# Gate stage of a streaming encoder step: h added by accumulating transfers, upper frames transposed by VectorE

## The chip, the core and the metric

The kernel runs on one core of one Trainium2 chip. A core has five engines with a queue of instructions each, which they work off strictly in order: TensorE (PE; matmuls, 128 x 128), VectorE (DVE), ScalarE (ACT), GpSimd (POOL) and SyncE (SP), and 16 DMA engines that move data between the on-chip memory (SBUF) and the device's memory. Matmuls write to PSUM, from which VectorE and ScalarE read. Transfers are issued by an engine's queue: here by SP, POOL and, for a few, ScalarE. The metric is the device time of one execution in microseconds, the median of the runs; the profile is of one more execution.

## What is computed

One layer of an encoder on 2048 prompt frames and 32 sample frames of width 1024. The part that matters here is the last step, the gate, and the norm behind it:

```
hn = rmsnorm(h, g_mix);  proj = hn @ w_in;  ... two mixers ...
h = h + concat[yA, yB] @ w_out
gate = sigmoid(rmsnorm(h, g_ple) @ w_ple_gate)
h = h + (p @ w_ple) * gate
y = rmsnorm(h, g_final)
```

Everything is in 32-bit floats. Each 32-bit operand of a product is split into a high and a low part, and three matmuls (high x high, high x low, low x high) make one exact enough.

## The kernel before

**Stages.** The projections and mixers run first, then the output product with `w_out`, which writes the new h to memory (`h_d`), then, from about 704 us, nine embedding products `p @ w_ple`, which write e to memory (`e_d`), and from about 729 us the gate. In the stretch of the embedding products the gate's weights are prepared by VectorE and ScalarE.

**Tiles and pairs.** h is cut into 16 tiles of 128 rows and one of 32. The gate takes the tiles in pairs (0 and 1, 2 and 3, ... 14 and 15). For a pair the product 256 x 1024 by 1024 x 1024 is cut into 2 x 2 blocks and done with seven block products in place of eight (`seven`, L273). Each of the seven is 12 matmuls of 128 x 512. The products accumulate in three PSUM banks X, Y and Z; between them ScalarE copies a bank aside (`carry`, L1571), and `out` (L1576) adds the copy back, takes the sigmoid on ScalarE with the row's norm factor `rs_h` as its scale, and multiplies it with e on VectorE. The order of products in a pair: X with block 11 (carry), Y with 12 (out of the upper left quarter), X with S2 (carry), Z with S1 (carry), X with S3 (out of the lower right), Z with S4 (out of the upper right), X with 22 (out of the lower left). The tile of the upper rows is complete after the sixth product, that of the lower rows after the seventh. A product that accumulates on a bank must wait until the carry or the sum before it has read that bank.

**Frames.** The products want h turned, with its columns on the partitions. `prep_g(i)` (L1732) makes the frames of a pair: the turned blocks a11, a12 (upper tile) and a21, a22 (lower tile), their combinations S1 to S4 (`comb`), and the high and low parts of seven of them (`put`, through `split`, L80: a cast on ScalarE and a subtraction on VectorE). The lower tile is read in quarters (`by_quarters`, L1507: four transfers of 32 rows, so that the four 32-row groups lie where a transpose of 32 x 32 blocks gives the turned tile) and turned in place by one VectorE instruction (`turned_here`, L1558). The upper tile is read by rows (`load_rows`, L393) and turned by `turned` (L1544): two copies on ScalarE, which put the columns in the same order, and eight transposes on TensorE into PSUM. The frames of pair i+2 are made while pair i is multiplied, at steps between the products (`following`).

**Closing a tile.** `out` adds e * gate onto the tile of h, which has been read from `h_d`. `done_g` (L1589) then sums the squares on ScalarE (`sumsq`, L92), has POOL compute the factor (two small instructions, `rstd_of`, L70), multiplies on VectorE and stores. The last pair (`last_pair`, L1613) has a handwritten end of its own and its own loads of h.

**Order.** The kernel's code gives a program order; a scheduler with its own estimates of durations orders the instructions within each engine's queue, apart from those pinned by `keep_in_program_order`. Tiles come from rings: `ya` has five buffers of 128 x 1024, `xh` four, `st` four of 128 x 512, `ss` three. A tile's load waits until the tile that had its buffer before is no longer read. Before the change `ya` holds the frames' rows and e, `xh` holds h.

## Time and profile before

| what | value |
|---|---|
| median of 3 runs | 909.32 us (908.84 to 909.93) |
| the profiled execution | 909.97 us, of which the span of the profile is 908.2 us |
| granted TensorE clock | 0.998 of full speed |
| TensorE busy 729.4 to 895.9 us (the gate) | all of it |
| transposes on TensorE | 72: 64 of 128 rows and 8 of 32 rows (the short tile) |

The profile tells for each engine when it was busy, in what line of the kernel, and for the idle time before an instruction which other engine or transfer ended it last. A busy TensorE alone does not say that it is the bound; the chain of waits does. It goes back from the last instruction to what released each step, and here it stays on TensorE from the output product to 899.75 us, with a tail of some 8 us on the other engines and the last stores. In names such as `x_g<-wg,g` the first is the PSUM bank, then the weights and the frames; `pth` is the bank of the transposes, `c_g` a carried copy.

### The profile page before, as it was taken

What the parts mean: (1) busy time and instruction counts of PE and PEld (TensorE: products, weight loads), DVE (VectorE), ACT (ScalarE), POOL (GpSimd) and SP (SyncE); (2) the same over time, 40 slices, a digit from 0 to 9 for tenths busy, and PEclk for the clock granted to TensorE, in tenths of its full rate; (3) what the DMA queues carried; (4) which work ended last, traced back from release to release, by engine and by line L of the source; (5) the groups of instructions that cost most, each with busy time, mean ns of one, the idle gap of its engine ahead of it and who ended that gap; (6) DMA issues with size and microseconds to landing.
All of it is one profiled execution on the core that took longest, in us unless ns stands there. A gap on an engine that the chain in (4) does not pass through costs nothing.

```text
span 908.2 us, 12176 instructions
## 1 busy us (share of the span) xinstructions
PE 893.2 (98%) x4174; PEld 722.8 (80%) x4174; DVE 702.4 (77%) x1158; ACT 460.1 (51%) x834; POOL 152.0 (17%) x290
## 2 busy tenths in 40 slices
PE   8999999999999999999999999999999999999996
PEld 6788888888888887877778886888887888778885
DVE  6899799897993688846667579965565988897885
ACT  7744554554453345533444376544434865565554
POOL 2210122222121123100000020221111211120012
PEclk9999999999999999999999999999999999999999
DMA  8255286857699666667745496787677965565554
GB/s 268 63 188 172 84 262 204 246 157 226 179 340 424 176 222 200 215 222 225 264 136 175 163 331 198 255 259 250 199 274 254 342 244 176 184 228 196 185 193 168
DMA packets 113387, 198.52 MB, mean 219 GB/s; under 512 B 13174, under 2 KB 70062, under 8 KB 112429
## 3 DMA queue, kind: packets, MB, share of 16 engines
q1 hardware_dynamic: 91309, 124.72, 42.5%
q0 software_dynamic: 19568, 68.62, 22.2%
q10 hardware_dynamic: 2448, 4.39, 1.3%
q8 instruction: 33, 0.54, 0.3%
q14 instruction: 29, 0.24, 0.1%
HBM read 132.53 MB, written 65.15 MB: 218 GB/s over the span
## 4 chain that ended last, share of the span: by engine, by line
PE 73%; issue 11%; DMA 8%; DVE 3%; ACT 2%; POOL 2%; POOLq 0%; DVEq 0%; ACTq 0%
PE x_g L185 9%; PE x_o L185 8%; PE x_zab L646 6%; PE x_zbv L646 6%; PE x_ch L646 6%; PE z_g L185 5%; PE z_o L185 4%; DMA raw_zab_0b<-in_w_in_dram 4%; PE z_zab L646 3%; PE z_ch L646 3%; PE z_zbv L646 3%; PE e L109 2%; PE y_g L185 2%; PE y_o L185 2%; DMA B<-p_d 2%
## 5 line engine op out<-in xcount | busy, mean ns | idle before, releaser
L185 PE MATMUL z_o<-wo,y_S 128*128 128x512 f32 x192 | 47.4, 389 | 0.0
L185 PE MATMUL x_o<-wo_T,y_S 128*128 128x512 f32 x192 | 46.4, 391 | 0.6 <-DVE c_o L1319 0.6
L646 PE MATMUL x_zab<-B,w_zab_S 128*128 128x512 f32 x192 | 46.8, 392 | 0.2 <-DVE w_zab_S L84 0.2
L185 PE MATMUL z_g<-wg,g_S 128*128 128x512 f32 x192 | 46.8, 391 | 0.0
L646 PE MATMUL z_zab<-B,w_zab_S 128*128 128x512 f32 x192 | 46.8, 391 | 0.0
L185 PE MATMUL x_o<-wo,y 128*128 128x512 f32 x192 | 45.2, 390 | 0.0
L646 PEld LDWEIGHTS x_zab<-B,w_zab_S 128*128 128x128 f32 x192 | 35.8, 188 | 8.8 <-DVE w_zab_S L84 0.6
L185 PEld LDWEIGHTS x_o<-wo_T,y_S 128*128 128x128 f32 x192 | 35.9, 188 | 8.7 <-DVE c_o L1319 1.3
L185 PEld LDWEIGHTS x_o<-wo,y 128*128 128x128 f32 x192 | 36.1, 188 | 7.7
L646 PEld LDWEIGHTS z_zab<-B,w_zab_S 128*128 128x128 f32 x192 | 35.8, 188 | 7.8 <-DVE w_zab_S L84 0.3
L185 PEld LDWEIGHTS z_o<-wo,y_S 128*128 128x128 f32 x192 | 36.0, 188 | 7.5
L646 PE MATMUL x_ch<-B,w_ch_S 128*128 128x512 f32 x168 | 41.9, 393 | 0.0
L185 PEld LDWEIGHTS z_g<-wg,g_S 128*128 128x128 f32 x192 | 35.8, 188 | 7.5 <-ACT c_g L1573 0.2
L646 PE MATMUL x_zbv<-B,w_zbv_S 128*128 128x512 f32 x168 | 40.9, 393 | 0.3 <-ACT zs L986 0.3
L646 PE MATMUL z_zbv<-B,w_zbv_S 128*128 128x512 f32 x168 | 40.5, 390 | 0.0
L646 PE MATMUL z_ch<-B,w_ch_S 128*128 128x512 f32 x168 | 40.4, 390 | 0.0
L646 PEld LDWEIGHTS x_zbv<-B,w_zbv_S 128*128 128x128 f32 x168 | 31.3, 188 | 8.0 <-ACT zs L986 0.7
L646 PEld LDWEIGHTS x_ch<-B,w_ch_S 128*128 128x128 f32 x168 | 31.3, 188 | 7.3 <-ACT U L986 0.4
L646 PEld LDWEIGHTS z_ch<-B,w_ch_S 128*128 128x128 f32 x168 | 31.6, 188 | 6.6
L646 PEld LDWEIGHTS z_zbv<-B,w_zbv_S 128*128 128x128 f32 x168 | 31.5, 188 | 6.5
L81 ACT CAST y_S<-y_fS 128x512 fp32r<-128x512 f32 x28 | 17.0, 620 | 28.1 <-PE x_o L185 12.2
L1319 DVE TENSOR_TENSOR c_o<-x_o,x 128x512 f32<-128x512 f32 x14 | 9.6, 689 | 21.8 <-PE x_o L185 21.8
(552 smaller groups left out, 2288.9 us busy)
## 6 DMA issues: line engine op xcount, KB each, us to landing
wn<-in_w_in_dram SPq DMA_DIRECT2D x24, 512.0 KB, 4.8
y<-y_d SPq DMA_DIRECT2D x16, 512.0 KB, 6.8
p_dT<-T POOLq DMA_DIRECT2D x15, 512.0 KB, 5.1
e<-e_d SPq DMA_DIRECT2D x15, 512.0 KB, 4.1
x<-in_x_prompt_dram SPq DMA_DIRECT2D x14, 512.0 KB, 5.6
B<-p_d POOLq DMA_DIRECT2D x3, 2048.0 KB, 15.6
B<-p_dT POOLq DMA_DIRECT2D x3, 2048.0 KB, 21.5
h_d<-x SPq DMA_DIRECT2D x12, 512.0 KB, 7.1
```

The source lines that it names most:

```text
L81: ins = nc.scalar.copy(hi, src)
L109: nc.tensor.matmul(ps, pps[:, a, k], wp[k][b][:, cs], start=k + q == 0, stop=k == 1 and q == 2)
L185: nc.tensor.matmul(ps[:n], lhs[:, k, a, :n], w[b][:, k], start=start and k + q == 0, stop=k == KH - 1 and q == 2, skip_group_check=True)
L646: nc.tensor.matmul(ps, lhs[:, k, x], b[:, k, y], start=start and k + q == 0, stop=stop and k == KH - 1 and q == 2, skip_group_check=True)
L1319: add = lambda o, a, b: nc.vector.tensor_tensor(o, a, b, op=ALU.add)
```

## The change

- h is no longer loaded for the pairs ahead of the last. `out` multiplies e by the gate in place, and when a tile's second half is done, an accumulating transfer on POOL's queue adds the tile's rows of `h_d` onto e. The 28 additions of these tiles on VectorE go.
- `done_g` of a pair's two tiles works on e, and moves into the next pair: at its step 4 (after product four) for the upper tile, at step 6 for the lower one; in the last pair at steps 3 and 4. The sum of squares and the multiplication are pinned there.
- e is read into `ya` (the first pair's into `xh`), the frames from tile 4 on into `xh`, and the frames' reads come at step 1.
- The upper tile is read in quarters too and turned by VectorE, pinned in program order. The 64 transposes on TensorE and the 16 copies on ScalarE go.
- The stores of tiles 6 to 11 move from SP's queue to POOL's.

```diff
-        def by_quarters(i):
+        def by_quarters(i, pool=ya):
             r, n = tiles[i]
-            t = ring4(ya, f"hn_{i}")
+            t = ring4(xh if i > 3 else pool, f"hn_{i}")
...
-            first_h = load_rows(xh, "hn", 0, h_d)
+            first_h = by_quarters(0, xh)
...
-                ee, hh = half_of(e, at, n), half_of(h, at, n)
+                ee = half_of(e, at, n)
                 nc.vector.tensor_tensor(ee, ee, c[:n], op=ALU.mult)
-                nc.vector.tensor_tensor(hh, hh, ee, op=ALU.add)
+                if h is not None:
+                    hh = half_of(h, at, n)
+                    nc.vector.tensor_tensor(hh, hh, ee, op=ALU.add)
+                elif at[0] + at[1] == 1:
+                    r = tiles[i + at[0]][0]
+                    nc.gpsimd.dma_start(e[at[0]], h_d[r:r + P], accum_op=ALU.add)
...
-            nc.vector.scalar_tensor_tensor(h[:n], h[:n], rf[:n], g_bc[:n], op0=ALU.mult, op1=ALU.mult)
-            (nc.sync if 6 <= i < NT - 1 else nc.gpsimd).dma_start(rows_of(y_p, y_s, r, n), h[:n])
+            ins = nc.vector.scalar_tensor_tensor(h[:n], h[:n], rf[:n], g_bc[:n], op0=ALU.mult, op1=ALU.mult)
+            if later:
+                tc.keep_in_program_order(ins)
+            (nc.sync if NT - 5 <= i < NT - 1 else nc.gpsimd).dma_start(rows_of(y_p, y_s, r, n), h[:n])
...
-            seven(f"g{i}", A, W, held, out, {1: chunk, 3: before, 4: rest, 5: upper_half}, first_tile=True, end=end)
+            seven(f"g{i}", A, W, held, out, {1: chunk, 3: sooner, 4: lambda: (before(), rest()), 5: upper_half}, first_tile=True, end=end)
...
-                got["upper"] = load_rows(ya, "hn", i, h_d) if i else first_h
+                got["upper"] = by_quarters(i) if i else first_h
...
+            def sooner():
+                if not ahead:
+                    load()
+
             def first():
-                if not ahead:
+                if not got:
                     load()
-                lower.extend(turned_here(got["lower"], not i))
+                lower.extend(turned_here(got["lower"], True))
...
-                a11, a12 = turned(i, got["upper"])
+                a11, a12 = turned_here(got["upper"], True)
...
-            return {2: first, 4 if i in (2, 8) else 3: second}
+            return {1: sooner, 2: first, 4 if i in (2, 8) else 3: second}
...
+        def joined(a, b):
+            def both(p, q):
+                def run():
+                    p()
+                    q()
+                return run
+            return {**a, **{st: both(a[st], f) if st in a else f for st, f in b.items()}}
...
-            h = [load_rows(xh, "h", i + b, h_d, queue=nc.gpsimd if i < 6 else nc.sync) for b in range(2)]
-            e = [load_rows(ya, "e", i + b, e_d) for b in range(2)]
-            seven(f"g{i}", A, W, *gate_ops(h, e, P, f"g{i}", i), following)
-            done_g(i, h[0])
+            e = [load_rows(ya if i else xh, "e", i + b, e_d) for b in range(2)]
+            if i:
+                following = joined(following, finish)
+            seven(f"g{i}", A, W, *gate_ops(None, e, P, f"g{i}", i), following)
+            finish = {st: lambda b=b, i=i, e=e: done_g(i + b, e[b], True) for b, st in enumerate((4, 6))}
             if i in (0, 2, 4):
                 next(short_steps)
-            if i + 2 < NT - 3:
-                done_g(i + 1, h[1])
-        last_pair(NT - 3, S[NT - 3], lambda: done_g(NT - 4, h[1], True))
+        last_pair(NT - 3, S[NT - 3], finish[4], finish[6])
```

How this moves instructions is seen at three places. In names like `g12_S2` the first number is the pair's upper tile. First TensorE, in the pair of tiles 10 and 11, from the fifth product on; before:

```order
L185 MATMUL x_g10_7546<-wg_T3_6494,g10_S3_7451 128x512 x12
L185 MATMUL z_g10_7548<-wg_21_6507,g10_S4_7454 128x512 x10
L1554 MATMUL pth_12_0_7603<-ident_75,ho_12_0_7604 128x128 x4
L1554 MATMUL pth_12_1_7610<-ident_75,ho_12_1_7611 128x128 x4
L185 MATMUL z_g10_7548<-wg_21_6507,g10_S4_7454 128x512 x2
L185 MATMUL x_g10_7546<-wq_6245,g10_22_7457 128x512 x12
```

and now:

```order
L185 MATMUL x_g10_7436<-wg_T3_6484,g10_S3_7346 128x512 x12
L185 MATMUL x_g12_7604<-wg_11_6219,g12_11_7496 128x512 x2
L185 MATMUL z_g10_7438<-wg_21_6497,g10_S4_7349 128x512 x12
L185 MATMUL x_g10_7436<-wq_6245,g10_22_7352 128x512 x12
L185 MATMUL x_g12_7604<-wg_11_6219,g12_11_7496 128x512 x10
```

The eight transposes are gone, and two matmuls of the next pair's first product stand ahead of the sixth product.

Second VectorE, in the pair of tiles 12 and 13, from the sum of its fifth product on; before:

```order
L1581 TENSOR_TENSOR c_g12_11_7840<-x_g12_7730,c_g12_11_7840 128x512
L1584 TENSOR_TENSOR e_13_7728<-e_13_7728,c_g12_11_7840 128x512
L1585 TENSOR_TENSOR h_13_7724<-h_13_7724,e_13_7728 128x512
L1560 STREAM_TRANSPOSE hn_15_7763<-hn_15_7763 128x1024
L1581 TENSOR_TENSOR c_g12_01_7783<-z_g12_7732,c_g12_01_7783 128x512
L1743 TENSOR_TENSOR g14_fS1_7785<-hn_15_7763 128x512
L1584 TENSOR_TENSOR e_12_7726<-e_12_7726,c_g12_01_7783 128x512
L84 TENSOR_TENSOR g14_11_7801<-pth_14_0_7787,g14_11_7801 128x4x128
```

and now:

```order
L1581 TENSOR_TENSOR c_g12_11_7703<-x_g12_7604,c_g12_11_7703 128x512
L84 TENSOR_TENSOR g14_S4_7685<-g14_fS4_7677,g14_S4_7685 128x4x128
L1581 TENSOR_TENSOR c_g12_01_7659<-z_g12_7606,c_g12_01_7659 128x512
L84 TENSOR_TENSOR g14_22_7688<-hn_15_7621,g14_22_7688 128x4x128
L1597 SCALAR_TENSOR_TENSOR e_10_7432<-e_10_7432,rstd_f10_7709,g_bc_89 128x1024
L1584 TENSOR_TENSOR e_13_7602<-e_13_7602,c_g12_11_7703 128x512
L1584 TENSOR_TENSOR e_12_7600<-e_12_7600,c_g12_01_7659 128x512
L1584 TENSOR_TENSOR e_13_7602<-e_13_7602,g_g12_10_7764 128x512
L1597 SCALAR_TENSOR_TENSOR e_11_7434<-e_11_7434,rstd_f11_7748,g_bc_89 128x1024
```

The frames of the next pair (the two transposes, the combinations and all but two of the splits) now stand ahead of the sum of the fifth product, and the multiplications that complete the tiles 12 and 13 come behind all of them and behind the closing of tile 10. The accumulating transfers follow the last two of these multiplications.

Third ScalarE, at the start of the last pair; before:

```order
L94 ACTIVATE junk_90,ssq_f12_7890<-h_12_7722 128x1024
L1573 COPY c_g14_01_7961<-x_g14_7908 128x512
L94 ACTIVATE junk_90,ssq_f13_7963<-h_13_7724 128x1024
L1666 ACTIVATE c_g14_00_7923<-c_g14_00_7923,rs_h_88 128x512
L1573 COPY c_g14_11_7983<-z_g14_7910 128x512
L1638 ACTIVATE junk_90,ssq_l0_0_7985<-h_14_7902 128x512
```

and now:

```order
L1673 ACTIVATE c_g14_00_7793<-c_g14_00_7793,rs_h_88 128x512
L1573 COPY c_g14_01_7831<-x_g14_7778 128x512
L94 ACTIVATE junk_90,ssq_f12_7833<-e_12_7600 128x1024
L1573 COPY c_g14_11_7853<-z_g14_7780 128x512
L94 ACTIVATE junk_90,ssq_f13_7855<-e_13_7602 128x1024
L1645 ACTIVATE junk_90,ssq_l0_0_7863<-h_14_7772 128x512
```

The squares of tile 12 stand between the copies of the third and of the fourth product, those of tile 13 behind the latter, and both read a tile that a transfer has completed.

More of the change, by code (lines that the diff above doesn't have):

```diff
@@ L1611, in short_ops, with last_pair @@
             return carry, out
-        def last_pair(i, A, before):
+        def last_pair(i, A, sooner, before):
             pps = load_pps(ss.tile([P, 2, 2, P], F32R, tag="s", name="pps_l"), i + 1, nc.sync)
@@ L1739, in put, with comb @@
                 split(view(A[q][:, :, 0]), view(A[q][:, :, 1]), src)
-            def comb(q, x, y, op, view=lambda t: t):
-                t = ss.tile([P, KH, P], F32, tag="s", name=f"g{i}_f{q}")
-                nc.vector.tensor_tensor(view(t), x, y, op=op)
+            def comb(q, x, y, op):
+                t = whole(ss.tile([P, KH, P], F32, tag="s", name=f"g{i}_f{q}"))
+                nc.vector.tensor_tensor(t, x, y, op=op)
                 return t
@@ L1749, in load, with first @@
                 got["lower"] = by_quarters(i + 1) if i else first_lower
-                got["upper"] = load_rows(ya, "hn", i, h_d) if i else first_h
+                got["upper"] = by_quarters(i) if i else first_h
             if ahead:
                 load()
-            def first():
+            def sooner():
                 if not ahead:
                     load()
-                lower.extend(turned_here(got["lower"], not i))
+            def first():
+                if not got:
+                    load()
+                lower.extend(turned_here(got["lower"], True))
             def second():
                 a21, a22 = lower
-                s1 = comb("S1", a21, a22, ALU.add, whole)
-                a11, a12 = turned(i, got["upper"])
-                put("11", a11)
+                s1 = comb("S1", a21, a22, ALU.add)
+                a11, a12 = turned_here(got["upper"], True)
+                put("11", a11, whole)
                 s2 = comb("S2", s1, a11, ALU.subtract)
-                s3 = comb("S3", whole(a11), a21, ALU.subtract, whole)
-                put("12", a12)
-                put("S2", s2)
+                s3 = comb("S3", a11, a21, ALU.subtract)
+                put("12", a12, whole)
+                put("S2", s2, whole)
                 s4 = comb("S4", a12, s2, ALU.subtract)
-                put("S1", s1)
-                put("S3", s3)
-                put("S4", s4)
+                put("S1", s1, whole)
+                put("S3", s3, whole)
+                put("S4", s4, whole)
                 put("22", a22, whole)
             S[i] = A
-            return {2: first, 4 if i in (2, 8) else 3: second}
+            return {1: sooner, 2: first, 4 if i in (2, 8) else 3: second}
         S = {}
```

## The prediction

> **What bounds the kernel now.** I read the page's busy table, then the chain of waits over the last 200 us in order of time. The chain (start, length, what) runs on TensorE without a break through the whole gate stage; this is the pair of tiles 6 and 7, then the first, the slowest and the last of the eight groups of transposes, and the last product:
>
> ```profile
> PE 893.2 (98%) x4174; PEld 722.8 (80%) x4174; DVE 702.4 (77%) x1158; ACT 460.1 (51%) x834; POOL 152.0 (17%) x290
> ...
> 718.71 0.87 PE pth L1554 x8
> ...
> 781.61 2.72 PE x_g L185 x12
> 784.33 0.46 PE z_g L185 x2
> 784.78 0.88 PE pth L1554 x8
> 785.66 2.31 PE z_g L185 x10
> 787.97 2.72 PE x_g L185 x12
> ...
> 854.06 1.03 PE pth L1554 x8
> ...
> 876.65 0.87 PE pth L1554 x8
> ...
> 899.75 0.73 PE e_l L109 x6
> ```
>
> A product of twelve matmuls takes 2.72 us, seven of them 19.04 us a pair, and a transpose group is simply wedged between them. So what TensorE no longer does comes off the end, as long as the other engines keep feeding it. The next view, busy time by stretches (length, then PE, PEld, DVE, ACT, POOL busy with counts, clock, DMA share, GB/s), says how much room they have: the stretch in which the embedding product hides the gate's weights, and one pair of the gate:
>
> ```profile
> 704.00:729.40 25.40, 25.40 (x117) 20.55 (x117) 24.83 (x40) 22.37 (x45) 7.23 (x15) 1.00 0.95 334
> ...
> 836.00:858.00 22.00, 22.00 (x102) 18.11 (x101) 18.95 (x28) 11.89 (x21) 2.07 (x4) 1.00 0.53 191
> ```
>
> VectorE is at 18.95 of 22 us in a pair, ScalarE at 11.89, and the transfers use about half of their engines. VectorE is the second bound, three microseconds a pair behind.
>
> **Removed from TensorE.** Eight groups of eight 128-row transposes leave it (the eight 32-row ones of the short tile stay). Six of the groups took 0.87, one 0.88, one 1.03: together 7.1 us, all on the chain. Nothing is added there. This is the whole gain on offer.
>
> **VectorE and ScalarE.** The groups by line over the gate stage:
>
> ```profile
> L1585 DVE TENSOR_TENSOR h<-h,e 128x512 f32<-128x512 f32 (+1 forms) x30 | 20.0, 684 | 0.8 <-DMA h<-h_d 0.6
> L1560 DVE STREAM_TRANSPOSE hn<-hn 128x1024 f32<-128x1024 f32 x8 | 9.9, 1238 | 0.0
> L1552 ACT COPY ho<-hn 128x512 f32<-128x512 f32 (+1 forms) x18 | 10.4, 619 | 3.4 <-DMA hn<-h_d 3.4
> ```
>
> 28 of the 30 additions go. Back to back they come every 0.60 us (two of them in a row of 1.28 below), so 2.4 us a pair. One more transpose a pair costs 1.24. VectorE is relieved by about 1.2 us a pair, TensorE's pair shrinks by 0.9: the room stays what it was. ScalarE loses two copies a pair, 16 of the 18. Both are off the chain and I count them at zero.
>
> In the embedding stretch VectorE is full (24.83 of 25.40), and there the added transpose has no removed addition beside it: all that follows is 1.2 us later. What would be late next is the lower weights' splits, which the second product wants. In the new order they stand behind the frames of the first pair; counted at 0.6 us each they end some 4 us before that product starts. Zero, and at worst 1.2 us if that cover is gone.
>
> **Order inside a pair.** This is the place where the new order is tighter. Old pair of tiles 8 and 9:
>
> ```profile
> 827.00 0.69 DVE L1584 TENSOR_TENSOR e<-e,c_g 128x512 f32<-128x512 f32 x1 [0.79 <-ACT c_g L1582]
> 827.61 1.24 DVE L1560 STREAM_TRANSPOSE hn<-hn 128x1024 f32<-128x1024 f32 x1
> ...
> 829.34 0.68 DVE L1743 TENSOR_TENSOR g_fS<-hn 128x512 f32<-128x512 f32 x1
> 832.74 0.69 DVE L84 TENSOR_TENSOR g<-pth,g 128x512 fp32r<-128x512 f32 x1 [2.71 <-ACT g L81]
> ...
> 834.05 1.66 ACT L81 CAST g_S<-g_fS 128x512 fp32r<-128x512 f32 x3 [0.86 <-DVE g_fS L1743]
> ...
> 841.14 1.28 DVE L1585 TENSOR_TENSOR h<-h,e 128x512 f32<-128x512 f32 x2
> ...
> 844.61 1.28 DVE L1592 SCALAR_TENSOR_TENSOR h<-h,rstd_f,g_bc 128x1024 f32<-128x1024 f32 x1 [0.17 <-POOL rstd_f L77]
> ```
>
> VectorE used to wait 2.71 us for TensorE's and ScalarE's turn of the upper frames; now it runs two transposes and nine operations in one go. From a pair's start: product two ends at 5.4, its sum, sigmoid and multiplication end at about 7.7, two transposes and nine operations take 2 x 1.24 + 9 x 0.60 = 7.9, and the sum of product five ends at 16.3. Product seven accumulates on that bank and starts at 16.3 plus whatever of the next pair's first product is put before it (2 to 11 matmuls). Just in time. On ScalarE, in the pairs of tiles 10 and 12, five casts now stand ahead of the copy of product four that product six waits for: cast one starts when the upper transpose ends, about 10.8, five at 0.52 apiece (three in a row of 1.66 with its tail) end at 13.4, the copy at 14.0, product six is due at 13.6 plus two matmuls, 14.1. I take 0.3 us for each of these two pairs: 0.6. Lower bound zero, upper bound 1 us in each of seven pairs.
>
> **The transfers.** The 14 loads of h become 14 accumulating transfers, all on POOL's queue, and each is now behind a multiplication and ahead of a tile's statistics. The nearest rows (last number: median us from issue to landing) are plain loads of the same size, and the quarters that the upper frames now use too:
>
> ```profile
> h<-h_d POOLq DMA_DIRECT2D x6, 512.0 KB, 5.2
> ...
> hn<-h_d SPq DMA_DIRECT2D x25, 128.0 KB, 2.9
> ...
> L396 POOL DMA_DIRECT2D h<-h_d x6: 527/532/577, 729.3 to 781.0; - x6
> ```
>
> No accumulating transfer is in this trace. Below, it lands like a plain load: 5.2. Above, it reads both operands and takes twice that: 10.4. The fixed part of the 5.2 is not doubled, so I take the middle, 7.8. The quarters cost nothing: they are read a pair ahead, 2.9 us each, into a ring that e no longer shares. On SP's queue a load of e now waits for the store of the tile five before it, and quarters stand behind it; by the order that store ends early in the pair before the one that wants the tile, over 10 us ahead. Behind a waiting accumulation on POOL stand the statistics and the store of the pair before, which are wanted only by the ring.
>
> When is it wanted? VectorE's order puts the multiplication that completes a pair's first tile about 20.5 us after that pair's start, 1.5 into the next; with 0.53 of issue it starts at 2.0. In the middle pairs its squares stand behind the copy of product four, at about 14.5: 12.5 us of room. In the last pair they stand behind the copy of product three:
>
> ```profile
> 886.52 0.59 ACT L1573 COPY c_g<-x_g 128x512 f32<-128x512 f32 x1 [1.33 <-PE x_g L185]
> 887.01 1.06 ACT L94 ACTIVATE junk<-h 128x1024 bf16<-128x1024 f32 x1
> ...
> 889.24 0.57 ACT L1573 COPY c_g<-z_g 128x512 f32<-128x512 f32 x1
> 889.89 2.97 PE L185 MATMUL z_g<-wg,g_S 128*128 128x512 f32 x12
> ```
>
> There that is 9.0 us after the pair's start, 7.0 of room. The second pair is as tight: the first pair's multiplication stands behind frames that started late behind the weights, some 6 us into the second pair by the same counting; its squares are due at 11.5, and the casts behind them have about 1.2 more before a product waits: 6.7, call it 7. What queues behind a late square on ScalarE is the copy of product four (last pair) or the frames' casts (second pair), and TensorE waits for both. I price each at landing time less 7: 0.8 twice, 1.6 us.
>
> The Trainium skill ("Collectives: The Full Stack", the bandwidth ceiling) says that an add in the transfer is slow not for the add but because it reads two sources, and gives about half the rate. By "DMA: Bandwidth & Descriptors" (anatomy of one DMA) a plain one of 512 KB would be 2.0 plus 1.2 us; doubling the second term gives an estimate of 4.4 in all, and the 1.6 us would be zero. The loads here show 5.2, so its fixed part is too small in this traffic, and no run here shows the add.
>
> **The sum.** Profiled execution 909.97 (span 908.20, 1.77 around it): 909.97 - 7.1 + 0.6 + 1.6 = 905.1. That execution lies 0.65 above the median of the runs, 909.32, so the forecast for the median is 904.4.
>
> **Rivals.** (a) The transfer lands within 7 us: only the 0.6 is lost, 902.8. For it: DMA engines half idle in the stage, and the plain loads' 5.2. Against it: two operands. By the skill's two pages this is the outcome. (b) Slower: the accumulating transfers land late. Each microsecond above 7 costs two in all, and above 12.5 also one in each of five middle pairs; 6.5 us of gain are gone at 10.3, and 0.2% is lost at about 11.2. At 14 us it is 909.3 - 6.5 + 14 + 7.5 = 924. For it: POOL's loads of h under the heavy traffic before the stage took a median of 9.3, and issue is serial with statistics and stores on POOL's queue. Against it: DMA share 0.53 in a pair.
>
> ```profile
> h<-h_d POOLq DMA_DIRECT2D x2, 512.0 KB, 9.3
> ```
>
> (c) No change: VectorE's unbroken run makes the sum of product five late by a microsecond in each of the seven pairs, and TensorE waits for it where it used to transpose: 909.3 - 7.1 + 7 = 909. For it: the margin above is nearly nothing. Against it: the next pair's matmuls that the order puts ahead of product seven, up to 2.5 us of cover. That the transposes stay is no rival: in the order of the changed kernel the 128-row ones are gone.
>
> **How the numbers follow.** Forecast 0.50 (903.2 to 907.5), (a) 0.25, (b) 0.13, (c) 0.12. A measurement of this kernel can tell about 0.2%, 1.8 us. Forecast and (a) are both faster: 0.75; (c) is the same: 0.12; (b) slower: 0.13. The range starts at full gain, 902.0, and reaches through (c) to 909.5; left out is (b).
>
> **What would show it.** Right: no 128-row transposes on TensorE and products of 2.72 us back to back; accumulating transfers landing within 6 to 9 us; TensorE's gaps, if any, at product six of the last pair and in the second pair, with squares of e as ScalarE's wait on a transfer. Wrong: landing times above 10 us and ScalarE waiting on them in every pair (b), or TensorE's product seven waiting for VectorE's sums (c), or a gap before the gate's first products, behind the weights' splits.

## The result, and the profile after

| | before | changed |
|---|---|---|
| median | 909.32 us (908.37 to 911.04, 7 runs) | 915.30 us (911.28 to 916.38, 7 runs) |
| ratio, 95% interval | | 1.0056 (1.0036 to 1.0075) |
| the profiled execution, and its span | 909.97, 908.2 | 916.35, 914.6 |
| TensorE's last product ends at (row start plus length) | 900.47 | 907.68 |

The change makes the kernel slower by about 0.6%, where 904.4 us was forecast. TensorE has lost its transposes and still ends 7.2 us later. The first view says where: what TensorE waited for in the whole execution (total, times, longest).

```profile
...
PE x_gl L337 <- DVE c_gl L1608: 2.3, 1, 2.3
PE x_g L1722 <- DVE c_g L1677: 2.0, 1, 2.0
PE e L109 <- ACT eout L167: 2.0, 1, 2.0
PE x_g L185 <- DVE c_g L1581: 1.4, 2, 0.9
...
PE z_g L185 <- ACT c_g L1573: 1.0, 1, 1.0
```

Before, TensorE was busy through all of the gate. Now it waits at six places from the embedding products on; the rows left out lie ahead of them. The timeline of TensorE (start, length, line, operation, count, and in brackets the wait before) has five of them in the gate: in the pair of tiles 2 and 3, at the short tile between the pairs 4 and 6, in the pair 6, and twice in the last pair:

```profile
772.95 3.03 PE L185 MATMUL x_g<-wq,g 128*128 128x512 f32 x12 [0.54 <-DVE c_g L1581]
...
801.70 1.14 PE L337 MATMUL x_gl<-wg,gl_a 128*64 128x512 f32 x4 [2.27 <-DVE c_gl L1608]
802.64 1.91 PE L340 MATMUL x_gl<-wg,gl_a 128*32 128x512 f32 x4
...
823.21 3.01 PE L185 MATMUL x_g<-wq,g 128*128 128x512 f32 x12 [0.87 <-DVE c_g L1581]
...
894.80 3.01 PE L185 MATMUL z_g<-wg,g_S 128*128 128x512 f32 x12 [0.99 <-ACT c_g L1573]
...
903.02 1.69 PE L1722 MATMUL x_g<-wq,g 128*128 128x256 f32 x12 [2.04 <-DVE c_g L1677]
```

Behind the wait of 2.27 us a step of four small matmuls took 1.91 us; the same step took 1.09 elsewhere. The reason stands in the view by windows (length, busy time of PE, PEld, DVE, ACT and POOL with counts, then the granted TensorE clock, DMA share and GB/s):

```profile
802.00:804.00 2.00, 2.00 (x8) 0.92 (x7) 2.00 (x4) 0.01 (x1) 0.00 (x0) 0.65 1.08 342
804.00:806.00 2.00, 2.00 (x6) 1.58 (x5) 1.37 (x4) 0.58 (x1) 0.56 (x1) 0.50 0.96 194
```

The granted clock is at one half from about 802.6 to 806, from 0.9 us behind the end of the wait. That costs 0.35 x 2 + 0.50 x 2 = 1.7 us on top of the wait. It happens once more, in the stretch of the embedding products. TensorE's timeline of before, then that of after:

```profile
704.94 13.77 PE L109 MATMUL e<-wq,pps 128*128 128x512 f32 x60
...
729.48 2.90 PE L185 MATMUL x_g<-wg,g 128*128 128x512 f32 x12
```

```profile
706.08 8.32 PE L109 MATMUL e<-wq,pps 128*128 128x512 f32 x36
716.37 15.48 PE L109 MATMUL e<-wq,pps 128*128 128x512 f32 x60 [1.97 <-ACT eout L167]
...
733.53 1.77 PE L185 MATMUL x_g<-wg,g 128*128 128x512 f32 x7
```

From the first embedding product to the gate it was 24.54 us, of which 0.87 were transposes; now it is 27.45 without them. So 3.78 us are lost: the wait, and 1.7 at half clock behind it.

The sum for this execution: 3.78 here, 0.54 + 0.87 in two pairs, 2.27 + 1.7 at the short tile, 0.99 + 2.04 in the last pair, 12.2 us in all. The embedding products also started 1.14 later, from work ahead of them; over the sixteen profiles here this start lies between 703.67 and 707.76 us, and the lowest is that of a repeat of the changed kernel, so it is not the change's. 12.2 + 1.14 - 7.1 = 6.2 of the 7.2 us. Of the last 1.0 some 0.8 can be estimated: rows of 2.88 us follow each other every 2.72, and this overlap of 0.16 is missing at each of the five waits in the gate. The tail after the last product is 0.8 shorter (6.92 in place of 7.73).

The transfers of after, from issue to landing (the page's last part: queue, count, size, median us), and the group of their issues on POOL (busy, mean ns):

```profile
hn<-h_d SPq DMA_DIRECT2D x65, 128.0 KB, 7.4
...
e<-e_d SPq DMA_DIRECT2D x15, 512.0 KB, 7.6
...
e<-h_d POOLq DMA_DIRECT2D x14, 512.0 KB, 8.3
```

```profile
L1590 POOL DMA_DIRECT2D e<-h_d x14 | 13.1, 935 | 22.3 <-DVE e L1584 21.8 <-issue 0.4
```

The accumulating transfers land after 8.3 us, where 7.8 was forecast. What was not forecast is that the loads beside them became slower too: e from 4.1 to 7.6, the quarters from 3.0 to 7.4. The addition is only a part of this: in the experiments below, e took 6.0 and the quarters 5.9 with plain copies in its place, and 5.9 and 3.4 with the addition but without the upper quarters.

In the last pair the chain can be read off the timelines of POOL (the issues for tiles 12 and 13), ScalarE and VectorE, in this order:

```profile
883.85 0.90 POOL L1590 DMA_DIRECT2D e<-h_d  x1 [0.18 <-issue]
...
884.97 1.22 POOL L1590 DMA_DIRECT2D e<-h_d  x1
```

```profile
893.12 1.06 ACT L94 ACTIVATE junk<-e 128x1024 bf16<-128x1024 f32 x1 [2.26 <-DMA e<-h_d]
...
896.90 1.06 ACT L94 ACTIVATE junk<-e 128x1024 bf16<-128x1024 f32 x1 [2.15 <-DMA e<-h_d]
```

```profile
899.00 1.29 DVE L1597 SCALAR_TENSOR_TENSOR e<-e,rstd_f,g_bc 128x1024 f32<-128x1024 f32 x1 [2.48 <-POOL rstd_f L77]
...
902.28 0.69 DVE L1677 TENSOR_TENSOR c_g<-x_g,c_g 128x512 f32<-128x512 f32 x1
```

The squares of tile 12 start when its transfer has landed, 9.3 us after the issue began, those of tile 13 11.9 us after theirs. The copy of product four stands behind the former, at 894.18: TensorE's 0.99. The closing multiplication of tile 13 is pinned on VectorE ahead of the sums of products six and five, and waits 2.48 for its factor. The last product waits for the second of these sums: 2.04.

In the second pair (tiles 2 and 3) it is the same kind of chain, on ScalarE and then on VectorE:

```profile
766.90 1.06 ACT L94 ACTIVATE junk<-e 128x1024 bf16<-128x1024 f32 x1 [2.58 <-DMA e<-h_d]
```

```profile
768.59 1.30 DVE L84 TENSOR_TENSOR g<-hn,g 128x512 fp32r<-128x512 f32 x2 [3.75 <-ACT g L81]
...
772.21 0.69 DVE L1581 TENSOR_TENSOR c_g<-x_g,c_g 128x512 f32<-128x512 f32 x1
```

The squares of tile 0 wait 2.58 for its transfer, the casts of the next frames stand behind them, VectorE waits 3.75 for the casts, and the sum of product five comes behind its splits. That is TensorE's 0.54.

### The profile page after: what moved, and what is told of

The parts are those of the page before. It is cut to its first block, busy times and chain, and to the rows that moved or that the text cites. A ratio compares the mean times of both kernels' runs of the same rounds, so it can differ in the third digit from the quotient of the medians.

```text
span 914.6 us, 12059 instructions
## 1 busy us (share of the span) xinstructions
PE 890.8 (97%) x4110; PEld 718.0 (79%) x4110; DVE 695.2 (76%) x1138; ACT 452.8 (50%) x818; POOL 166.9 (18%) x304
## 5 line engine op out<-in xcount | busy, mean ns | idle before, releaser
L81 ACT CAST y_S<-y_fS 128x512 fp32r<-128x512 f32 x28 | 17.0, 620 | 26.7 <-PE x_o L185 11.9
L1373 POOL DMA_DIRECT2D gs<-in_w_ple_gate_dram x16 | 11.5, 716 | 88.2 <-DMA g_d<-gs 33.8
```

The lines of the kernel that those rows point to most:

```text
L81: ins = nc.scalar.copy(hi, src)
L1373: ins = nc.gpsimd.dma_start(t, rows[:, :, half * NH:half * NH + NH])
```

## The experiments

Each kernel was timed beside the kernel before on the same chip. Ratios are to the kernel before, with 95% intervals; the changed kernel stands at 1.006.

| run | median us | ratio |
|---|---|---|
| again (the change, repeated) | 916.73 | 1.0060 (1.0036 to 1.0083) |
| accum_only | 918.32 | 1.0087 (1.0071 to 1.0102) |
| turn_only | 933.04 | 1.0248 (1.0231 to 1.0266) |
| plain_copy | 910.14 | 0.9990 (0.9973 to 1.0007) |
| first_rows | 914.12 | 1.0034 (1.0021 to 1.0048) |
| late_done | 916.22 | 1.0052 (1.0036 to 1.0068) |
| last_plain | 913.49 | 1.0027 (1.0012 to 1.0042) |
| halves | 912.05 | 1.0004 (0.9985 to 1.0023) |
| combo_rows | 910.96 | 0.9998 (0.9985 to 1.0010) |
| combo_late | 914.60 | 1.0034 (1.0018 to 1.0051) |
| combo_plain | 909.80 | 0.9983 (0.9967 to 0.9999) |
| combo_plain_2 (the same, later) | 909.76 | 0.9991 (0.9980 to 1.0002) |
| sum_first | 906.63 | 0.9958 (0.9942 to 0.9975) |
| sum_only | 915.72 | 1.0056 (1.0034 to 1.0077) |

### The two halves of the change, and the price of the accumulation

**accum_only**: h by accumulating transfers, the upper tiles by rows and TensorE as before.

```diff
-            first_h = by_quarters(0, xh)
+            first_h = load_rows(xh, "hn", 0, h_d)
...
-                got["upper"] = by_quarters(i) if i else first_h
+                got["upper"] = load_rows(xh if i > 3 else ya, "hn", i, h_d) if i else first_h
...
-                a11, a12 = turned_here(got["upper"], True)
+                a11, a12 = map(whole, turned(i, got["upper"]))
```

> h added by accumulating transfers as in the change, but all upper tiles read by rows and turned by TensorE, as before. Theory A: the embedding stretch is as before (no loss of 3.8), the last pair still waits for the transfers of tiles 12 and 13 (3.0), the second pair for 0.5, and VectorE has 2.4 us a pair less to do: about 909.3 + 3.5 = 913. Theory B (accumulating transfers slow everything by their doubled traffic): all the losses of the change stay and the 7.1 us of transposes come back, 920 or more. Theory C (the quarters do it): 909 to 910.

918.32, between theories A and B. Its embedding stretch took 24.53 us, as before the change. TensorE's waits in the gate:

```profile
782.29 1.12 PE L1554 MATMUL pth<-ident,ho 128*128 128x128 f32 x4 [3.50 <-ACT ho L1552]
903.21 2.12 PE L1722 MATMUL x_g<-wq,g 128*128 128x256 f32 x12 [1.90 <-DVE c_g L1677]
```

Two waits of 5.4 us together; the clock stood at one half for some 7 us around the end of the first (781.3 to 788.2) and 3.5 behind the second. The last pair's wait is there without any upper quarters, so it does not need them. Theory C falls. The first wait is one that the changed kernel does not have: ScalarE waits for rows of h that are late. SyncE stood for 3.8 us before their read, until a tile of e was stored. So 918.32 is not a clean price of the accumulation; it has this detour through the ring `xh` in it.

**turn_only**: the kernel before, with upper tiles in quarters and turned by VectorE (pinned in the first pair alone, as the lower tiles were). The combinations and splits follow the new layout.

```diff
-            first_h = load_rows(xh, "hn", 0, h_d)
+            first_h = by_quarters(0, xh)
...
-                got["upper"] = load_rows(ya, "hn", i, h_d) if i else first_h
+                got["upper"] = by_quarters(i) if i else first_h
...
-                a11, a12 = turned(i, got["upper"])
+                a11, a12 = turned_here(got["upper"], not i)
```

> Upper tiles read in quarters and turned by VectorE, but h loaded and added by VectorE as before. Theory A: 909.3 - 7.1 for the transposes + 3.8 in the embedding stretch + 0 to 3 where VectorE (now 1.2 us a pair fuller than before) is late: 906 to 909. Theory B: without accumulating transfers the whole gain comes, 902 to 903. Theory C (the 28 more quarters and VectorE's long run do it): 913 to 916.

933.04: no theory had this. TensorE waits for frames at the start of each of the last five pairs, once for 8.51 us. TensorE's timeline there, then VectorE's just before:

```profile
849.12 1.22 PE L185 MATMUL x_g<-wg,g 128*128 128x512 f32 x2 [8.51 <-ACT g L81]
```

```profile
845.97 1.28 DVE L1592 SCALAR_TENSOR_TENSOR h<-h,rstd_f,g_bc 128x1024 f32<-128x1024 f32 x1 [0.72 <-POOL rstd_f L77]
847.17 1.24 DVE L1560 STREAM_TRANSPOSE hn<-hn 128x1024 f32<-128x1024 f32 x1
```

VectorE turns the next pair's upper tile only after it has closed both tiles of this pair. So in the old order the turning costs far more than it saves. In the changed kernel the closings have moved into the next pair, the transposes are pinned ahead of them, and the 28 additions are gone; which of these saves it was not tried apart. The two halves of the change don't add: 0.9% and 2.5% slower alone, 0.6% together.

**plain_copy**: the 14 transfers without the addition; e times the gate is missing from tiles 0 to 13.

```diff
-                    nc.gpsimd.dma_start(e[at[0]], h_d[r:r + P], accum_op=ALU.add)
+                    nc.gpsimd.dma_start(e[at[0]], h_d[r:r + P])
```

> The 14 accumulating transfers become plain ones of the same size from the same queue at the same place (e times the gate is left out of tiles 0 to 13, h's rows overwrite it). Prices the accumulation itself. Theory B: issue falls from 0.89 to 0.53 us and landing from 8.3 to about 5.2, the last pair loses its waits, 911 to 912 us. Theory A': the landing is set by the traffic around it and by where the multiplications stand in VectorE's order: landing 7 us or more, time within 1.5 us of 915.3.

Its landing, its issues on POOL, and TensorE's waits at the short tile and at the last product:

```profile
e<-h_d POOLq DMA_DIRECT2D x14, 512.0 KB, 6.0
```

```profile
L1590 POOL DMA_DIRECT2D e<-h_d x14 | 7.7, 549 | 21.8 <-DVE e L1584 21.2 <-issue 0.4
```

```profile
795.94 1.12 PE L337 MATMUL x_gl<-wg,gl_a 128*64 128x512 f32 x4 [0.33 <-DVE c_gl L1608]
...
893.96 1.69 PE L1722 MATMUL x_g<-wq,g 128*128 128x256 f32 x12 [1.00 <-DVE c_g L1677]
```

The addition alone costs 0.7% (0.9990 against 1.0060), some 6 us: landing 8.3 against 6.0, issue 935 ns against 549, the short tile's wait 2.27 against 0.33, the last pair's 3.03 against 1.23 (0.23 and 1.00), the second pair's 0.54 against none (ScalarE's squares wait there for 0.52 in place of 2.58). In theory B's favour, and a little beyond it, though the landing fell less than it said. Even so the plain copy only draws level with the kernel before, and most of the 7.1 us of the transposes is missing there too: in its profile 1.36 by a later start of the embedding products, 0.58 in their stretch, 0.89 in the pair 6, and the waits above.

### The embedding stretch

**first_rows**: tile 0 by rows in one transfer, turned by TensorE.

```diff
-            first_h = by_quarters(0, xh)
+            first_h = load_rows(xh, "hn", 0, h_d)
...
-                a11, a12 = turned_here(got["upper"], True)
+                a11, a12 = turned_here(got["upper"], True) if i else map(whole, turned(0, got["upper"]))
```

> All as in the change, but the upper tile of the first pair is read by rows in one transfer and turned by TensorE, as before. Theory A (the gain is lost at single places where one transfer lands late; the biggest is the embedding stretch, where four quarters of tile 0 hold up SyncE's queue and the saturated transfers): the gate starts about 3.8 us earlier, less 0.9 for the transposes that come back, so about 912.4 us, 2.9 below the changed kernel's 915.3. Theory B (the stretch is late for what was late ahead of it, or the accumulating transfers slow all the rest): within 1 us of 915.3, or up to 0.9 above it.

914.12; the ratio fell by 0.0026, theory A's direction and most of its size, though the intervals overlap. The stretch itself is clearer than the total: 25.22 us in the profile, of which 0.87 are transposes, against 27.45. The wait at the short tile went too. In its place this execution has one of 3.11 us in the pair 6, with half clock behind it.

**again**: the changed kernel once more.

> The changed kernel once more, to see which of its stalls come in every execution. Theory A: the stalls before the short tile's product and in the last pair are there again with 0.5 us of the same place; the one in the embedding stretch (2.1 us and a stretch at half clock) may be missing, since a kernel with plain copies in place of the accumulations and the same quarters lost only 0.4 there. Rival (the quarters of the first pair always cost it): 2 us or more in the embedding stretch again. Time 914 to 916.

TensorE's timeline of this execution, at the embedding products and the last product:

```profile
713.17 13.88 PE L109 MATMUL e<-wq,pps 128*128 128x512 f32 x60 [1.17 <-DMA pps<-pp_d]
...
898.16 2.38 PE L1722 MATMUL x_g<-wq,g 128*128 128x256 f32 x12 [2.13 <-DVE c_g L1677]
```

The short tile's wait and the last product's are there again, 2.50 and 2.13 in place of 2.27 and 2.04, and the other three too, within 0.7 us; that in the embedding stretch is 1.17, and no half clock follows it. Nor does one follow the 2.50 this time; it follows the 2.13 of the last pair (2.38 us for a product of 1.69). Here the profile names a load of the embedding inputs, `pps`, as what ended that wait; in the first profile it names a copy of ScalarE. Of the nine profiles with tile 0 in quarters, six name the load and three the copy.

Taking all profiles together: the time from the first embedding product to the gate, less 0.87 where TensorE transposes there, was 23.66 to 24.35 us in the seven executions that read tile 0 by rows (before, accum_only, first_rows, and four of the combinations), and 24.20 to 28.27 in the nine that read it in quarters: 0.5 to 4.6 above the 23.67 of the kernel before, 2.7 on average. So quarters cost this stretch between half a microsecond and nearly five, from one execution to another.

SyncE's queue shows how (start, length, operation, count), before and then after:

```profile
700.15 0.40 SPq L396 DMA_DIRECT2D hn<-h_d  x1
700.64 18.41 SPq L129 DMA_DIRECT2D pps<-pp_d  x6
```

```profile
700.92 2.38 SPq L1512 DMA_DIRECT2D hn<-h_d  x4
704.87 16.43 SPq L129 DMA_DIRECT2D pps<-pp_d  x5
```

Before, the embedding products start at 704.94, and the next loads of their inputs go out from 4.3 us ahead of that. After, they start at 706.08, and these loads go out from 1.2 us ahead: they stand behind four issues in place of one, and SyncE then waits, between them, for loads of weights to land (its waits from 699 to 723 us, none of them there before):

```profile
SPq L129 <- DMA wg_b<-g_d: 3.9, 2, 2.0
SPq L129 <- DMA wq<-wl_d: 2.4, 2, 1.5
```

In all seven profiles with rows the lead is 4.1 to 4.7 us, in the eight with quarters at this place 0.0 to 1.2. How much of it TensorE then loses depends on when the loads land.

### The last pair

**late_done**: the closings of tiles 12 and 13 behind the sums of products five and six.

```diff
-... {1: chunk, 3: sooner, 4: lambda: (before(), rest()), 5: upper_half}, ...
+... {1: chunk, 4: rest, 5: lambda: (sooner(), upper_half()), 6: before}, ...
```

> In the last pair the closing of tile 12 moves behind the sum of the fifth product and that of tile 13 behind the sixth; all else as in the change. Theory A (the transfers of tiles 12 and 13 land later than what stands behind them can bear): both stalls of the last pair go, 0.99 before product four and 2.04 before the last product, and the half-clock stretch that follows such a stall in some executions, 3 to 4.5 us: 911 to 912.5. Rival (VectorE is late in the last pair anyway): the stalls stay within 0.5 us, 915, or the tail grows by the two multiplications that move back, 1.28 each: up to 917.

In its profile the last pair waits for 0.83 in place of 3.03, as theory A had it. The time did not follow: 916.22. That profile, the slowest of its eleven executions, lost 4.5 us in the embedding stretch, and 2.29 with half clock at the short tile. Whether the median hides a gain behind such losses, or the moved work costs it again in the tail, this run does not tell.

**last_plain**: h loaded and added by VectorE for tiles 12 and 13.

```diff
+            h = [load_rows(xh, "h", i + b, h_d) for b in range(2)] if i == NT - 5 else None
-            seven(f"g{i}", A, W, *gate_ops(None, e, P, f"g{i}", i), following)
-            finish = {st: lambda b=b, i=i, e=e: done_g(i + b, e[b], True) for b, st in enumerate((4, 6))}
+            seven(f"g{i}", A, W, *gate_ops(h, e, P, f"g{i}", i), following)
+            finish = {st: lambda b=b, i=i, e=h or e: done_g(i + b, e[b], True) for b, st in enumerate((4, 6))}
```

> For tiles 12 and 13 alone h is loaded ahead and added by VectorE, as before; their closing stays at the changed place. Theory A: no wait on a transfer is left in the last pair, about 912, like the moved closing. Rival (VectorE's backlog is the cause, and two to four additions of 0.60 make it worse): 915 to 917.

913.49, 0.33% below the changed kernel: theory A's size, though the two intervals overlap a little. The last product's wait fell from 2.04 to 0.44; product six still waits 1.36 for the copy of product four.

**halves**: each transfer in two halves of columns, each issued behind its own multiplication.

```diff
-                elif at[0] + at[1] == 1:
+                else:
                     r = tiles[i + at[0]][0]
-                    nc.gpsimd.dma_start(e[at[0]], h_d[r:r + P], accum_op=ALU.add)
+                    nc.gpsimd.dma_start(ee, h_d[r:r + P, at[1] * NH:at[1] * NH + NH], accum_op=ALU.add)
```

> Each accumulating transfer is cut into its two halves of columns, and each half is issued as soon as its own multiplication is done, so that only 256 KB of a tile are late. Theory A (landing time is the price, and it goes with the bytes): the late half lands in about 5.5 us in place of 8.3, the last pair's stalls shrink by 2 us or more: 912 to 913. Rival (rate is not what makes them late: issue on POOL's queue at 0.89 us each and the traffic around do): the halves land after 7 us or more, time 915 to 918.

TensorE's wait at the short tile:

```profile
801.74 1.10 PE L337 MATMUL x_gl<-wg,gl_a 128*64 128x512 f32 x4 [0.65 <-DVE c_gl L1608]
```

912.05, 0.56% or some 5 us below the changed kernel, more than the 2 to 3 expected, though a half still lands only after 6.9 us: landing does not halve with the bytes. The gain is at the short tile (0.65) and in the second pair (no wait) more than in the last pair (1.90 and 0.84, 2.74 together, against 3.03). The profiled execution is one of the slowest of the twelve (915.95), with 4.6 us lost in the embedding stretch.

### Putting it together

**combo_rows** is halves + first_rows + late_done; **combo_late** has late_done too, and the quarters of tile 0 put among the loads of the weights; **combo_plain** is halves + first_rows + last_plain.

The edit of combo_late to the quarters:

```diff
         with tc.issue_after(second_pps.ins):
             bots = rows_of_weight(cmb, "wg_b", g_d, 1, range(2))[0]
+            first_h = by_quarters(0, xh)
         with tc.issue_after(embed_weight.ins):
             bots += rows_of_weight(cmb, "wg_b", g_d, 1, range(2, KH))[0]
-            first_h = by_quarters(0, xh)
```

> Three edits together: the accumulating transfers in halves of columns, tile 0 read by rows and turned by TensorE, the closing of tiles 12 and 13 moved behind the sums of the fifth and sixth product. Theory A (the stalls are separate and add up): halves alone stood at 1.0004 of the kernel before; 2 us come off in the embedding stretch (2.9 on average less 0.9 for the transposes) and 2 to 2.7 in the last pair: a ratio of 0.995 to 0.997, some 907 to 908 us beside 911. Rival (what is removed in one place is waited for at the next, as the moved closing alone showed): 0.999 to 1.003.

> As the first, but tile 0 stays in quarters and is turned by VectorE; its quarters are put on SyncE's queue among the loads of the embedding weights in place of behind them. Theory A (four issues behind the weights hold up the embedding inputs): the embedding stretch loses under 1 us, and the 0.9 us of transposes is kept: 0.994 to 0.997. Rival (quarters cost that stretch wherever they stand, by VectorE's work or by traffic): 0.998 to 1.003.

> As the first, but in place of the moved closing tiles 12 and 13 have h loaded and added by VectorE. Theory A: the same as the first within 0.2%. Rival (the additions keep VectorE late in the last pair, as the wait for copy four showed when this was done alone): 1 to 2 us above the first.

910.96, 914.60 and 909.80. The rows keep the embedding stretch at 24.54 us; the quarters in their new place lost 3.8 of it. That goes as the rival said, but it does not clear SyncE's queue. Two quarters now stand where a load of the embedding inputs stood (at 691.90 before, at 693.06 in the changed kernel), and this load goes out with the others:

```profile
693.34 1.33 SPq L1512 DMA_DIRECT2D hn<-h_d  x2
...
702.02 19.27 SPq L129 DMA_DIRECT2D pps<-pp_d  x6
```

TensorE waits 2.02 us at 713.63 until such a load has landed. So the quarters held up a load of the inputs at this place as well; no run has quarters that delay none. What is left in the middle pairs of combo_plain, on TensorE and, ahead of the second wait, on VectorE:

```profile
815.75 3.06 PE L185 MATMUL x_g<-wq,g 128*128 128x512 f32 x12 [1.80 <-DVE c_g L1581]
...
836.53 1.66 PE L185 MATMUL x_g<-wq,g 128*128 128x512 f32 x6 [1.40 <-DVE c_g L1581]
```

```profile
827.81 1.24 DVE L1560 STREAM_TRANSPOSE hn<-hn 128x1024 f32<-128x1024 f32 x1
...
835.79 0.68 DVE L1581 TENSOR_TENSOR c_g<-x_g,c_g 128x512 f32<-128x512 f32 x1
```

This is the mechanism of the prediction's rival (c), in two pairs: product six followed product five at 831.57, the sum of product five came at 835.79 behind the unbroken run, and product seven waited for it.

**sum_first** is combo_plain with the splits behind that sum in program order:

```diff
-            return {1: sooner, 2: first, 4 if i in (2, 8) else 3: second}
+            return {1: sooner, 2: first, 4 if i in (2, 8) else 3: second, 5: third}
```

where `third` holds the seven `put` and the combination S4 that were in `second`.

> The third combination (halves, tile 0 by rows, h loaded for tiles 12 and 13), and the splits of the next pair's frames moved behind the sum of product five in the program's order, so that VectorE makes that sum before the five splits and the combination S4. Theory A (what is left of the loss in the middle pairs is rival (c): VectorE's unbroken run makes that sum late): the waits of 1.80 and 1.40 us ahead of product seven in the pairs of tiles 6 and 8 go, the ratio falls from 0.9983 to 0.995 or less. Rival (the sum then stands behind a closing that waits for an accumulating transfer, or the splits come late for the next pair's first product): waits of 1 us or more at those products or at the first, ratio 0.998 to 1.003.

> The third combination again, as the kernel to compare with on the same chip. Expected: a ratio of 0.998 within 0.002, and waits above 1 us ahead of product seven in the pairs of tiles 6 and 8 again.

906.63, a ratio of 0.9958 against 0.9991 for the same kernel without the edit on the same chip: 0.3%, some 3 us. The waits shrank rather than went: 1.39 and 0.73, with a new one of 0.62 in the pair 10. One of 1.40 in the last pair, which combo_plain_2 has at product six, went as well. Together TensorE's waits in the gate fell from 4.63 to 3.42 us in the two profiles, so 1.2 of the 3 us are seen there. This version beats the kernel before by 0.4%, and the changed one by 1%.

**sum_only**: that edit alone on the changed kernel.

> The changed kernel with one edit alone: the splits of the next pair's frames behind the sum of product five in the program's order. Theory A (each loss is its own, so the edit takes away rival (c)'s share wherever it is made): the waits ahead of product seven in the pairs of tiles 2 and 6 (1.4 to 2.7 us together in two executions) and part of VectorE's backlog ahead of the short tile (2.3 to 2.5 us and a stretch at half clock) go; 3 to 5 us off, a ratio of 1.001 to 1.003 beside the changed kernel's 1.006. Rival (with whole-tile transfers the sum's place is taken by closings that wait for them): within 0.2% of 1.006.

1.0056: nothing gained, as the rival said. The sum is early in the order, but a closing stands ahead of it on VectorE, and in the pair 2 this closing waits for its factor, whose squares waited 2.60 us for the transfer:

```profile
766.82 1.28 DVE L1597 SCALAR_TENSOR_TENSOR e<-e,rstd_f,g_bc 128x1024 f32<-128x1024 f32 x1 [4.18 <-POOL rstd_f L77]
768.02 0.68 DVE L1581 TENSOR_TENSOR c_g<-x_g,c_g 128x512 f32<-128x512 f32 x1
```

TensorE waited 1.41 us there, with half clock behind it, and more than the changed kernel in the pairs 6 and 8 (1.15 and 1.27) and before the last product (2.72). The short tile's wait did go. So the edit alone is worth nothing, and 3 us beside three others. In the pair 2 it is the whole-tile transfer that takes the gain; in the pair 8 a closing waits for its factor in sum_first too (1.70 us), so how much each of the three edits adds stays open.

## Why the prediction was wrong

The step that failed is the pricing of what TensorE would wait for. The prediction set these losses at 2.2 us (0.6 and 1.6); in the profiled execution they were 12.2. Its price for the embedding stretch was zero, and 3.78 were lost there; the short tile had no price at all, and 3.97 were lost there; the last pair was priced at 0.8, and took 3.03. By the runs, the addition in the transfers costs some 6 us, and tile 0 in quarters 2.7 on average, less 0.9 for the transposes that it saves there.

- **7.1 us off TensorE**: right. The 128-row transposes are gone, and between the waits the products run back to back.
- **VectorE and ScalarE in the embedding stretch at zero, at worst 1.2 us**: wrong. The step looked at VectorE's added transpose alone. The cost came with the transfers: four issues in place of one on SyncE's queue, and the loads of TensorE's own inputs behind them go out some 3 us later. Measured 3.78, 1.39 in the repeat, 2.7 on average over nine executions. It is shown that reading tile 0 in quarters does it. That it does so through the later loads is read from the traces, and six of nine waits end with such a load; the traffic of the small pieces and VectorE's pinned transpose were not tried apart.
- **"The quarters cost nothing"**: wrong for that reason, and for a second one. They are read "into a ring that e no longer shares", says the prediction; but the frames from tile 4 on share `xh` with the first pair's e. So SyncE stood before quarters for the pair of tiles 6 and 7 until a tile of the first pair was closed and stored, and VectorE got one tile late (SyncE's waits from 770 to 804 us, then VectorE's timeline):

```profile
SPq L1512 <- DMA out_dram<-e: 5.7, 2, 4.3
```

```profile
791.22 1.25 DVE L1560 STREAM_TRANSPOSE hn<-hn 128x1024 f32<-128x1024 f32 x1 [1.85 <-DMA hn<-h_d]
...
800.87 0.68 DVE L1608 TENSOR_TENSOR c_gl<-x_gl,c_gl 32x512 f32<-32x512 f32 x1
```

  The short tile's sum then came at 800.87, behind this backlog and a closing at 797.75: 2.27 us. The prediction looked at the rings pair by pair and never at the short tile, which has two products and a sum to fit in between. Halves and the plain copy brought this wait to 0.65 and 0.33 with all quarters in place, so the late closing of the first pair is the likelier cause than the quarters; but it went in first_rows and sum_only too, so VectorE's backlog has more than one source. The chain through the ring is read from the trace and was not tried by itself.
- **0.6 us for the order inside a pair**: near in size, in another place. The prediction put it on ScalarE in the pairs of tiles 10 and 12; the wait came on VectorE's side in the pair of tiles 6, 0.87 us (1.50 in the repeat), behind the unbroken run. Rival (c) had the mechanism; it acted in one pair of seven.
- **Landing at 7.8, price landing less 7 at two places**: the median landing was close (8.3, and 7.6 to 8.0 in other kernels), though it was only the middle between two bounds. The second pair went as told, with the squares late and the casts behind them: 0.54 us (1.20 in the repeat) for the 0.8 forecast. But in the last pair, where it is wanted first, the landing took 9.3 and 11.9. The price there was 3.03 us. By the formula 9.3 costs 2.3, and it counted only what queues on ScalarE behind the squares of tile 12. Left out was that the closing multiplication of tile 13 is pinned on VectorE ahead of two sums that TensorE needs.
- **A wait costs what it lasts**: never written down, but every term was priced so. After some waits the granted clock was at one half for about 3.5 us, at 1.7 us each. Two such stretches make 3.4 of the 7.2 us here. The Trainium skill ("TensorE: Matmul & The Clock Gate", Part 1) says that the clock is gated by windows of about 3.4 us that run freely. The length agrees. It asks for an idle window of that length before the clock falls; here it fell after waits of 1.41 (sum_only), 1.90 (accum_only) and 2.27 us, and did not after 2.04, 2.50 (in the repeat) or 2.70 (turn_only). The measurement decides: a wait of about 2 us cost 2 in some executions and 4 in others, and no run here shows what decides it. This fits the spread: the changed kernel ran in 911.2 to 922.6 us with mean clocks of 0.998 down to 0.990, the kernel before beside it in 908.9 to 915.0 at 0.997 to 0.999.
- **Rivals**: (b), slower through late accumulations, came nearest in kind, but not by its condition: at 8.3 us it should have cost 2.6, and its break-even was at 10.3. What the addition costs by the runs is 6 us.

## What to carry to other kernels

When work leaves the bound engine, look for each place where that engine now has no slack, and price a wait there above its length: a stall of 2 us on TensorE cost up to 4. Look at the queues that issue its loads, too: four transfers where there was one put the loads behind them 3 us later. A transfer that adds lands late and is slow to issue; cut it up so that only the last piece is late, which gave 0.56% here, and check what stands behind its consumer on the other engines. Edits that each remove a stall do not add up one by one: the order that was worth 3 us beside three other edits was worth nothing alone.

## What the runs showed of the hardware that was not expected

- Half clock for some 3.5 us after stalls as short as 1.4 us, and not after others of 2.5 and 2.7 (above).
- An accumulating transfer of 512 KB landed in 8.3 us against 6.0 for a plain one at the same place, and POOL needed 935 ns against 549 to issue it. Cut to 256 KB it still took 5.7 to 6.9 us.
- At nearly the same rate the DMA engines were busier: in the gate their busy share rose from 0.58 at 199 GB/s (729.48 to 900 us) to 0.74 at 198 (733.5 to 906). In its own gate plain_copy had 0.71 at 209 GB/s, and accum_only 0.68 at 190, so neither the addition nor the upper quarters account for it alone.
